# One weight stream for the delta rule's inputs, queries and keys, splits traced one unit ahead, and the decay chain traced in pieces

## The chip, the cores and the metric

The kernel runs on one core of one Trainium2 chip. Its time is the device time of one execution in microseconds (us), lower is better. The engines are named as the profile names them: PE (TensorE, matrix products), DVE (VectorE), ACT (ScalarE), POOL (GpSimd) and SP (SyncE, which only issues transfers here). Each engine works through its own instructions in order and waits on semaphores for the others.

## The reference

Two transformer blocks run after each other on 256 tokens of width 2048, all in float32. The change touches the first block alone:

```python
mod = silu(c) @ w_ada + b_ada                    # 6 vectors of 2048: shift, scale, gate, twice
h = rmsnorm(x, norm_mix) * (1 + sc_a) + sh_a
p = h @ w_in                                     # 2048 x 9296
c_q, c_kv, k_pe, q_g, k_g, v_g, z, b_logit, a_logit, gate_logits = split(p)
# latent attention, 8 heads
q = (rmsnorm(c_q) @ w_uq)                        # 512 x 8*(128+64), the last 64 of a head rotated
kv = (rmsnorm(c_kv) @ w_ukv)                     # 512 x 8*(128+128): keys and values
y_a = causal_attention(q, kv, rope(k_pe)) @ w_o_mla
# gated delta rule, 8 heads, chunks of 64 tokens
q, k, v = silu(causal_conv4(concat(q_g, k_g, v_g)))
beta = sigmoid(b_logit); g = -exp(A_log) * softplus(a_logit + dt_bias); G = cumsum(g) in each chunk
u, w = solve(I + strict_lower(beta * k k^T * exp(G_i - G_j)), [beta * v, beta * k * exp(G)])
S_next = S * exp(G_last) + (k * exp(G_last - G))^T (u - w S); o = (q * exp(G)) S + attn (u - w S)
y_b = (rmsnorm(o) * silu(z)) @ w_o_gdn
x = x + gt_a * ((sigmoid(gate_a) * y_a + sigmoid(gate_b) * y_b) @ w_o)
h = rmsnorm(x, norm_ffn) * (1 + sc_f) + sh_f
x = x + gt_f * ((silu(h @ w_gate) * (h @ w_up)) @ w_down)      # hidden width 5632
```

The second block (convolution and neighbourhood attention, then a feed-forward part of width 8192) follows.

## The kernel before

**Tiles.** Activations are kept with features on the 128 partitions and 256 tokens along the row, as two halves HI and LO whose sum is the float32 value. Weights come as units of 128x1024 float32 (512 KB). `Stream.load` (line 255) issues the transfer of a unit into one of 6 buffers named `raw`; `Stream.ahead` splits it: ACT rounds it to `hi` (line 268), DVE subtracts to get `lo` (line 269). There are 3 `hi` and 3 `lo` buffers for all streams together. `Stream.next` hands out slices of a unit; when a unit is used up it splits the next one there and then, unless one is ready, and calls `pump`. A product of 128 output features takes one 128-wide slice for each 128 inputs, so a unit holds 8 such slices; `mm` (lines 289 to 291) makes three products of 256 columns from a slice, `mm2` (lines 302 to 305) one of 512 and one of 256.

**Order.** The program is traced as straight code. A scheduler then orders the instructions of each engine: among those that it holds ready it takes what was traced first, and a transfer takes a free buffer in the order in which transfers were traced. Two helpers set the trace order. `merge` runs several generators side by side: each yields a cost, and the one with the lowest sum goes next. `pump` advances a list of fillers by a rate per weight unit. The fillers make the modulation vectors: `ada_pe` on PE (line 413) for the first two vectors while the first product runs, `ada_vec` (line 433) for the others, on ACT (line 440), DVE (line 441) and POOL (line 443), from weights in `raw` buffers. One step of `ada_vec` handles one 512 KB unit.

**Stages that the change touches.** (1) The start: 20 products of ones (line 506), the inputs, and the first modulation. (2) The first product, lines 519 to 550: 96 units of stream `wk` in six groups of input rows, with the modulation of a group made during the group before at a rate of its own (`RATE0`, line 38), and a `drain` at each group's start. (3) The logits of the decays (`proj(pm, wq, h)`, 2 units of `wq`), then the decay chain, lines 568 to 618: some 35 tiny instructions on PE, DVE and ACT, each fed by the one before. (4) Four sections, lines 1010 to 1020. Heads are handled in pairs: `pair_in` makes 6 convolved inputs of the delta rule (2 units of `wq` each), `pair_mid` the chunk matrices and their inverse by a chain of small products and DVE steps, `pair_out` the recurrence, `queries` the queries and keys of the attention from streams `wuq` and `wuk`, `attend` the attention. Section 1 merges `pair_in(0)` with the latents (lines 852 to 864), the rotary tables, the values (stream `wuv`) and `queries(0)`; sections 2 to 4 merge `pair_mid(i)`, `pair_out(i-1)`, `pair_in(i+1)`, `queries(i+1)` and the attention of pair i. (5) The output products (streams `woab` and `wo`), with fillers at rate 1.1 (`RATES[4]`), and the first group of the feed-forward product (stream `wgu`) with the last four `ada_vec` at rate 0.62.

A pair's inputs `kq` also sit in a `raw` buffer, from `pair_in` to the end of `pair_mid`.

## Time and profile before

| | us |
|---|---|
| median of 3 runs | 2780.33 (2779.88 to 2781.22) |
| the profiled execution | 2776.44 |
| its span, first to last instruction | 2774.7 |

The chip's profiler records every instruction of one execution. A *window* sums the busy time of each engine in a stretch of the span. *Waits* say which engine sat idle before an instruction and which other instruction ended the wait. The *timeline* lists instructions in order of time. TensorE's clock has two levels, 2.4 and 1.2 GHz; the profile gives the granted share, 1.00 and 0.50, and a window's mean of it. Times are us from the span's start unless marked ns. A number behind an x counts instructions.

### The profile page before, as it was taken

How to read it: one execution, taken by the hardware profiler on the slowest of the kernel's cores; microseconds unless marked ns; L12 is line 12 of the kernel's file. 1: busy time of each engine (PE TensorE's matmuls, PEld its weight loads, DVE VectorE, ACT ScalarE, POOL GpSimd, SP SyncE). 2: the span in 40 equal slices, each digit the busy share in tenths (PEclk: the TensorE clock that was granted, in tenths of full speed). 3: DMA queues.
4: the chain of work that ended last, by engine and by line, in shares of the span. 5: the costliest groups of instructions: out<-in, count | busy, mean ns of one | idle time of the engine just before them, and what ended most of it. 6: DMA issues, size and time to landing. Idle time of an engine off the chain costs nothing.

```text
span 2774.7 us, 42925 instructions
## 1 busy us (share of the span) xinstructions
PE 2677.4 (96%) x16226; PEld 2275.6 (82%) x16226; DVE 1941.0 (70%) x3066; ACT 1379.0 (50%) x2218; POOL 361.1 (13%) x310
## 2 busy tenths in 40 slices
PE   8999989899989999999999999999989999999997
PEld 5667867777777888888888889888978888888886
DVE  4865687778787877666666689796776566665665
ACT  5334565556554655344434564456554444453453
POOL 0000032223243122000000040000450000000012
PEclk9999989999999999999999999999999999999999
DMA  8795765548787687555555555544545555555553
GB/s 307 275 348 194 256 218 189 170 143 276 268 285 259 212 274 265 189 189 186 190 188 189 189 183 183 190 153 136 184 136 190 190 188 190 187 189 190 189 190 122
DMA packets 171279, 572.19 MB, mean 206 GB/s; under 512 B 19008, under 2 KB 19264, under 8 KB 171072
## 3 DMA queue, kind: packets, MB, share of 16 engines
q1 hardware_dynamic: 164736, 557.92, 59.5%
q10 hardware_dynamic: 6336, 11.53, 1.2%
q8 instruction: 128, 2.10, 0.3%
q14 instruction: 79, 0.65, 0.1%
HBM read 563.07 MB, written 6.29 MB: 205 GB/s over the span
## 4 chain that ended last, share of the span: by engine, by line
PE 78%; DVE 8%; DMA 5%; ACT 3%; issue 3%; POOL 2%; SPq 0%; ACTq 0%; DVEq 0%; POOLq 0%
PE ps L303 17%; PE ps L302 17%; PE ps L305 17%; PE ps L324 4%; PE ps L325 4%; PE ps L326 4%; PE ps L291 3%; PE ps L289 3%; PE ps L290 3%; DVE lo L269 3%; DMA raw<-ada 3%; PE O L426 1%; ACT hi L268 1%; DMA raw<-adaf 1%; DVE raw L441 1%
## 5 line engine op out<-in xcount | busy, mean ns | idle before, releaser
L269 DVE TENSOR_TENSOR lo<-raw,hi 128x1024 fp32r<-128x1024 f32 x856 | 1086.3, 1270 | 453.0 <-ACT hi L268 438.9
L268 ACT ACTIVATE hi<-raw 128x1024 fp32r<-128x1024 f32 x856 | 904.6, 1057 | 787.7 <-PE ps L305 442.1
L303 PEld LDWEIGHTS ps<-H,lo 128*128 128x128 f32 x2816 | 531.2, 189 | 139.2 <-DVE lo L269 21.8
L303 PE MATMUL ps<-H,lo 128*128 128x256 f32 x2816 | 576.5, 281 | 13.1 <-DVE lo L269 12.7
L302 PE MATMUL ps<-H,hi 128*128 128x512 f32 x1408 | 561.9, 400 | 15.5 <-DVE H L340 7.2
L305 PE MATMUL ps<-H,hi 128*128 128x512 f32 x1408 | 557.6, 397 | 0.1
L303 PEld LDWEIGHTS ps<-G,lo 128*128 128x128 f32 x1968 | 369.1, 188 | 92.1 <-DVE lo L269 7.1
L303 PE MATMUL ps<-G,lo 128*128 128x256 f32 x1968 | 389.7, 279 | 5.1 <-DVE lo L269 5.1
L305 PE MATMUL ps<-G,hi 128*128 128x512 f32 x984 | 388.7, 396 | 0.0
L302 PE MATMUL ps<-G,hi 128*128 128x512 f32 x984 | 386.9, 396 | 0.4 <-DVE Y L1056 0.4
L302 PEld LDWEIGHTS ps<-H,hi 128*128 128x128 f32 x1408 | 269.0, 191 | 22.7 <-DVE H L340 8.2
L377 POOL TENSOR_TENSOR acc<-acc,th 128x256 f32<-128x256 f32 x90 | 106.9, 1195 | 1318.4 <-ACT th L380 1317.4
L443 POOL TENSOR_TENSOR ada<-ada,raw 128x512 f32<-128x512 f32 x112 | 182.0, 1625 | 720.9 <-DVE raw L441 601.8
L305 PEld LDWEIGHTS ps<-H,hi 128*128 128x128 f32 x1408 | 265.7, 189 | 2.9 <-DVE H L340 0.3
L302 PEld LDWEIGHTS ps<-G,hi 128*128 128x128 f32 x984 | 187.0, 190 | 1.7 <-issue 0.7
L305 PEld LDWEIGHTS ps<-G,hi 128*128 128x128 f32 x984 | 184.8, 188 | 1.0
L324 PE MATMUL ps<-hi,H 128*128 128x512 f32 x448 | 175.7, 401 | 3.5 <-ACT hi L268 2.9
L325 PE MATMUL ps<-lo,H 128*128 128x512 f32 x448 | 177.0, 395 | 1.1 <-DVE lo L269 1.1
L326 PE MATMUL ps<-hi,H 128*128 128x512 f32 x448 | 175.8, 392 | 0.0
L289 PE MATMUL ps<-H,hi 128*128 128x256 f32 x528 | 151.5, 287 | 0.0
L291 PE MATMUL ps<-H,lo 128*128 128x256 f32 x528 | 151.4, 287 | 0.0
L290 PE MATMUL ps<-H,hi 128*128 128x256 f32 x528 | 151.4, 287 | 0.0
(394 smaller groups left out, 3384.5 us busy)
## 6 DMA issues: line engine op xcount, KB each, us to landing
raw<-wdn SPq DMA_DIRECT2D x216, 512.0 KB, 3.3
raw<-wgu SPq DMA_DIRECT2D x176, 512.0 KB, 3.3
raw<-wup SPq DMA_DIRECT2D x128, 512.0 KB, 3.3
raw<-wk SPq DMA_DIRECT2D x96, 512.0 KB, 5.2
raw<-ada SPq DMA_DIRECT2D x96, 512.0 KB, 4.5
raw<-wo SPq DMA_DIRECT2D x64, 512.0 KB, 4.2
Y<-ada SPq DMA_DIRECT2D x112, 256.0 KB, 5.6
raw<-wq SPq DMA_DIRECT2D x50, 512.0 KB, 4.3
```

The costliest lines, as they stand in the source:

```text
L268: S.activation(hi[:, sl], raw[:, sl], AF.Copy)
L269: V.tensor_tensor(lo[:, sl], raw[:, sl], hi[:, sl].bitcast(F32), op=ALU.subtract)
L289: PE.matmul(out, wh, x[:, HI], start=first, stop=False)
L290: PE.matmul(out, wh, x[:, LO], start=False, stop=False)
L291: PE.matmul(out, wl, x[:, HI], start=False, stop=last)
L302: PE.matmul(out, wh, x, start=first, stop=False)
L303: PE.matmul(out[:, LO], wl, x[:, HI], start=False, stop=last and wide)
L305: PE.matmul(out, wh, x, start=False, stop=last)
L324: PE.matmul(out, x[:, h], wh, start=(i == 0), stop=False)
L325: PE.matmul(out, x[:, h], wl, start=False, stop=False)
L326: PE.matmul(out, x[:, l], wh, start=False, stop=(i == n - 1))
L443: G.tensor_tensor(s, s, a0, op=ALU.add)
```

## The change

- **One stream.** The weights of the query and key products (`w_uq`, the key half of `w_ukv`) are laid into the array of `wq`, behind the delta rule's inputs of the same pair of heads, in the order of use. Streams `wuq` and `wuk` are gone. In each section `queries` follows `pair_in` in one chain; in section 1 the chain is `pair_in(0)`, `values`, `queries(0)`, and beside it run the latents, the decay chain and the rotary tables.
- **One ahead.** When `Stream.next` takes up a unit and no other is ready, it traces the split of the next unit at once. That holds for all streams.
- **Fillers.** `ada_pe` and `ada_vec` trace the transfer of their next weights one step earlier. The first product has one rate, 0.85 steps per unit, for all groups, and at a group's start only so many steps are forced as its inputs need. `RATES[4]` goes from 1.1 to 1.0. The last four `ada_vec` run with `shared=False`: two DVE instructions a step, none on ACT and POOL.
- **Decays.** The decay chain becomes a generator with ten yields, merged into section 1.
- The 20 products of ones are removed.

```diff
-RATE0 = (1.7, 1.3, 1.3, 1.25, 1.25)
+RATE0 = 0.85
-RATES = (0.85, 0.85, 0.62, 1.8, 1.1, 3.5, 4.2, 2.3)
+RATES = (0.85, 0.85, 0.62, 1.8, 1.0, 3.5, 4.2, 2.3)
...
                 self.hi, self.lo = self.ready.pop(0)
                 self.i = 0
+                if not self.ready and self.u < self.src.shape[0]:
+                    self.ahead()
                 pump()
...
-    def ada_vec(stream, chunks):
+    def ada_vec(stream, chunks, shared=True):
...
             w = stream.unit()
+            if stream.u < stream.src.shape[0] and k < KT - 2:
+                stream.prefetch(1)
             a0, a1 = w[:, :512], w[:, 512:]
-            S.activation(a0, a0, AF.Copy, scale=cact[:, k:k + 1])
-            V.scalar_tensor_tensor(a0 if k else s, a1, cact[:, k + 1:k + 2], a0, op0=ALU.mult, op1=ALU.add)
-            if k:
-                G.tensor_tensor(s, s, a0, op=ALU.add)
+            c0, c1 = cact[:, k:k + 1], cact[:, k + 1:k + 2]
+            if shared:
+                S.activation(a0, a0, AF.Copy, scale=c0)
+                V.scalar_tensor_tensor(a0 if k else s, a1, c1, a0, op0=ALU.mult, op1=ALU.add)
+                if k:
+                    G.tensor_tensor(s, s, a0, op=ALU.add)
+            else:
+                if k:
+                    V.scalar_tensor_tensor(s, a0, c0, s, op0=ALU.mult, op1=ALU.add)
+                else:
+                    V.tensor_scalar(s, a0, c0, None, op0=ALU.mult)
+                V.scalar_tensor_tensor(s, a1, c1, s, op0=ALU.mult, op1=ALU.add)
...
-    warm = ps("ps")
-    for i in range(20):
-        PE.matmul(warm[:, :P], ones, ones, start=True, stop=True)
...
     for gi, ks in enumerate(KGROUPS):
-        drain()
+        while len(h) <= ks[-1]:
+            step()
...
-        if gi + 1 < len(KGROUPS):
-            nx = KGROUPS[gi + 1]
-            filler.append(ada_group(nx))
-            rate[0] = (4 * len(nx) if nx[0] < NS else 3 * len(nx)) / (6 * len(ks)) * RATE0[gi]
+            for nx in KGROUPS[1:]:
+                filler.append(ada_group(nx))
+            rate[0] = RATE0
...
-    wuv, wuq, wuk = Stream("wuv", 512), Stream("wuq"), Stream("wuk")
+    wuv = Stream("wuv", 512)
...
-        merge(pair_in(0), chain(latents(), rotary_tables(), shared_key(), values(), queries(0, todo[0])))
+        merge(chain(pair_in(0), values(), queries(0, todo[0])), latents(), decays(), chain(rotary_tables(), shared_key()))
...
-    merge(pair_mid(0), pair_in(1), *[attend(*t) for t in todo[0]], queries(1, todo[1]))
-    merge(pair_mid(1), pair_out(0), pair_in(2), *[attend(*t) for t in todo[1]], queries(2, todo[2]))
-    rate[0] = RATES[1]
+    merge(pair_mid(0), chain(pair_in(1), queries(1, todo[1])), *[attend(*t) for t in todo[0]])
+    merge(pair_mid(1), pair_out(0), chain(pair_in(2), queries(2, todo[2])), *[attend(*t) for t in todo[1]])
...
-        filler.append(ada_vec(ada1, [32 + 4 * q + i for i in range(4)]))
+        filler.append(ada_vec(ada1, [32 + 4 * q + i for i in range(4)], False))
```

How instructions stand on the engines around three places follows. A row is a line of the program, the operation, what it writes and reads (numbers are buffers), and the shape; the changed kernel's lines are its own.

PE behind the first product, before: the last slices of the second pair of `wq` units, then the decay chain's products and the transposes of the latents (L861).

```order
L302 MATMUL ps_3008<-H_1999,hi_3068 128x512
L303 MATMUL ps_3008<-H_1999,lo_3069 128x256
L303 MATMUL ps_3008<-H_2024,lo_3069 128x256
L305 MATMUL ps_3008<-H_2024,hi_3068 128x512
L596 MATMUL ax_2977<-g,const 128x16
L597 MATMUL ax_2977<-g,ones 128x16
L599 MATMUL ax_2980<-g,ones 128x16
L861 MATMUL ax_3034<-const,kk_177 128x128
L861 MATMUL ax_3034<-const,kk_178 128x128
```

The same place in the changed kernel (L885 is the transpose, L592 the first product of the decay chain):

```order
L307 MATMUL ps_2944<-H_1528,hi_2947 128x512
L308 MATMUL ps_2944<-H_1528,lo_2948 128x256
L885 MATMUL ax_2976<-const,kk_156 128x128
L592 MATMUL ax_2982<-const,Z_2922 128x128 x2
L885 MATMUL ax_2976<-const,kk_157 128x128
L885 MATMUL ax_2999<-const,kk_156 128x128
L885 MATMUL ax_2999<-const,kk_157 128x128
L308 MATMUL ps_2944<-H_1553,lo_2948 128x256
L310 MATMUL ps_2944<-H_1553,hi_2947 128x512
L885 MATMUL ax_3016<-const,kk_156 128x128
L885 MATMUL ax_3016<-const,kk_157 128x128
```

Before, 20 small products stood in a row behind the fourth unit; now they stand between slices of the fourth and fifth unit, and L596's successor comes after the fifth.

ACT at the same place, before: the split of the fourth unit (L268), then the decay chain (L575 to L582).

```order
L268 ACTIVATE hi730_3068<-raw729_3066 128x1024
L440 ACTIVATE raw732_3072<-raw732_3072,cact_69 128x512
L568 ACTIVATE Z708_2946<-ps704_2887 128x256
L575 ACTIVATE beta_2953<-lg_2951 128x16
L580 ACTIVATE ex_2957<-ab_2955 128x16
L582 ACT_TABLE_LOAD
L582 ACTIVATE ln_2959<-u_2958 128x16
L637 ACTIVATE th739_3113<-ps716_3008 128x256
```

In the changed kernel:

```order
L271 ACTIVATE hi713_2947<-raw712_2945 128x1024
L449 ACTIVATE raw715_2951<-raw715_2951,cact_69 128x512
L449 ACTIVATE raw734_3035<-raw734_3035,cact_69 128x512
L580 ACTIVATE Z707_2922<-ps703_2866 128x256
L271 ACTIVATE hi732_3031<-raw731_3029 128x1024
L612 ACTIVATE sm752_3125<-vec_63 128x8
L344 ACTIVATE Y722_2979<-ax721_2976,vec_63 128x256
L594 ACTIVATE beta_2925<-lg_2924 128x16
```

One more split, that of the fifth unit (hi732), stands ahead of the chain. The split after it stands 22 rows further down, behind the last table load, as the fifth unit's did before (24 rows).

PE in section 2, before: steps of `pair_mid` (L745 to L755) and of the attention (L947 to L956) of the first pair.

```order
L751 MATMUL ax_4041<-yi_3981,G_3941 64x64 x8
L755 MATMUL ax_4041<-G_3941,yi_3981 64x64 x8
L947 MATMUL ax_4074<-const,sa_3950 128x128 x2
L947 MATMUL ax_4079<-const,sa_3958 128x128 x2
L745 MATMUL ax_4087<-G_4058,G_3718 64x64 x8
L953 MATMUL ax_4099<-tx_3765,Y_3314 128x128
L954 MATMUL ax_4099<-tx_3765,Y_3314 128x128
```

In the changed kernel, the same steps (L769 to L779, L971):

```order
L769 MATMUL ax_3880<-G_3838,G_3696 64x64 x8
L307 MATMUL ps_3905<-H_854,hi_3862 128x512
L308 MATMUL ps_3905<-H_854,lo_3863 128x256
L308 MATMUL ps_3905<-H_883,lo_3863 128x256
L310 MATMUL ps_3905<-H_883,hi_3862 128x512
L307 MATMUL ps_3905<-H_1080,hi_3862 128x512
L775 MATMUL ax_3916<-yi_3879,G_3838 64x64 x8
L779 MATMUL ax_3916<-G_3838,yi_3879 64x64 x8
L308 MATMUL ps_3905<-H_1080,lo_3863 128x256
L971 MATMUL ax_3952<-const,sa_3847 128x128 x2
```

Products of the next pair's inputs (L307 to L310) now stand between steps that stood next to each other.

## Rows read from the trace of the kernel before

**Rows 1.** Windows: stretch, length; PE, PEld, DVE, ACT, POOL busy; clock, DMA share, GB/s.

```profile
27.30:343.80 316.50, 314.15 (x1458) 224.30 (x1458) 208.65 (x283) 136.66 (x171) 1.38 (x1) 1.00 0.76 267
355.60:375.40 19.80, 10.99 (x39) 7.31 (x40) 15.16 (x40) 13.82 (x25) 3.69 (x4) 0.57 0.14 44
375.40:666.70 291.30, 268.64 (x2120) 225.08 (x2120) 231.02 (x462) 173.85 (x434) 87.81 (x88) 0.98 0.59 200
666.70:897.00 230.30, 216.67 (x1311) 177.85 (x1309) 186.81 (x283) 120.97 (x194) 87.11 (x57) 0.99 0.77 274
908.00:1090.00 182.00, 176.66 (x1004) 150.63 (x1003) 149.29 (x194) 106.10 (x165) 43.45 (x28) 1.00 0.78 260
1090.00:1600.00 510.00, 510.00 (x2933) 445.06 (x2932) 315.56 (x401) 232.96 (x305) 2.31 (x2) 1.00 0.58 191
```

**Rows 2.** Timeline of PE, 340 to 400 us: start, us, line, shapes [idle before].

```profile
369.90 0.80 PE L302 MATMUL ps<-H,hi 128*128 128x512 f32 x1 [4.72 <-ACT hi L268]
```

**Rows 3.** Timeline of ACT, the same stretch.

```profile
346.77 1.06 ACT L268 ACTIVATE hi<-raw 128x1024 fp32r<-128x1024 f32 x1 [0.65 <-PE ps L290]
...
366.81 1.28 ACT L646 ACT_TABLE_LOAD   x1
...
368.81 1.04 ACT L268 ACTIVATE hi<-raw 128x1024 fp32r<-128x1024 f32 x1
```

**Rows 4.** Timeline of DVE, the same stretch.

```profile
346.91 0.16 DVE L348 TENSOR_SCALAR sm<-sm 128x4 f32<-128x4 f32 x1
...
369.88 1.23 DVE L269 TENSOR_TENSOR lo<-raw,hi 128x1024 fp32r<-128x1024 f32 x1 [0.44 <-ACT hi L268]
```

**Rows 5.** Waits of PE, 375.4 to 666.7 us: us in total, times, longest.

```profile
PE ps L303 <- DVE lo L269: 6.3, 8, 1.6
...
PE ps L291 <- DVE lo L269: 2.1, 3, 1.1
...
PE ps L302 <- ACT hi L268: 1.4, 1, 1.4
```

**Rows 6.** Waits of ACT, the same stretch.

```profile
ACT hi L268 <- PE ps L305: 16.8, 8, 4.3
```

**Rows 7.** Waits of PE, 666.7 to 897 us.

```profile
PE ps L303 <- DVE lo L269: 5.1, 4, 2.7
```

**Rows 8.** Waits of PE, 908 to 1090 us.

```profile
PE ps L303 <- DVE lo L269: 5.3, 9, 1.3
```

**Rows 9.** Groups of DVE by shape, 908 to 1090 us: busy, mean ns | idle before.

```profile
L269 DVE TENSOR_TENSOR lo<-raw,hi 128x1024 fp32r<-128x1024 f32 x61 | 90.2, 1479 | 9.0 <-ACT hi L268 8.0
L441 DVE SCALAR_TENSOR_TENSOR raw<-raw,cact 128x512 f32<-128x512 f32 x28 | 21.1, 752 | 16.8 <-ACT raw L440 16.8
L1093 DVE TENSOR_TENSOR tx<-tx,tx 128x256 f32<-128x256 f32 x15 | 11.8, 788 | 0.4
```

**Rows 10.** The same groups, 1200 to 1500 us.

```profile
L269 DVE TENSOR_TENSOR lo<-raw,hi 128x1024 fp32r<-128x1024 f32 x108 | 132.4, 1225 | 75.7 <-ACT hi L268 72.8
...
L1093 DVE TENSOR_TENSOR tx<-tx,tx 128x256 f32<-128x256 f32 x19 | 8.1, 425 | 0.7
```

**Rows 11.** Waits of ACT, 908 to 1090 us.

```profile
ACT raw L440 <- DMA raw<-ada: 47.0, 24, 4.2
```

**Rows 12.** Transfers, the page's part 6: KB each, median us from issue to landing.

```profile
raw<-wq SPq DMA_DIRECT2D x50, 512.0 KB, 4.3
```

**Rows 13.** Windows, the start: columns as in rows 1.

```profile
13.00:16.00 3.00, 2.70 (x26) 1.51 (x24) 1.34 (x8) 0.00 (x0) 0.00 (x0) 1.00 1.06 402
17.00:27.30 10.30, 7.27 (x25) 4.81 (x25) 3.78 (x8) 5.04 (x9) 0.00 (x0) 0.50 1.04 414
```

**Rows 14.** Timeline of PE: three small products, at the start and in section 1.

```profile
13.65 1.05 PE L389 MATMUL ax<-ones,H 128*128 128x1 f32 x8
...
19.12 1.01 PE L451 MATMUL ax<-vec,ada 128*128 128x1 f32 x4 [0.50 <-ACT ada L429]
...
386.47 1.05 PE L451 MATMUL ax<-ones,ada 128*128 128x1 f32 x8 [0.81 <-POOL ada L443]
```

More of the change, by code (lines that the diff above doesn't have):

```diff
@@ L411, in emit, with ada_pe @@
     cact = one("cact", (P, 16))
-    def ada_pe(stream, chunks):
+    def ada_pe(stream, chunks, more=False):
         n = P * len(chunks)
@@ L419, in ada_pe @@
                 yield
-            w = []
-            for g in range(4):
-                if n * g % stream.size == 0:
-                    w.append(stream.unit())
+            need = 4 * n // stream.size
+            w = [stream.unit() for _ in range(need)]
+            if k + 4 < KT or more:
+                stream.prefetch(need - len(stream.early))
             for g in range(4):
@@ L498, in ada_group @@
             for k in ks[::2]:
[L499 removed]
+                yield from ada_pe(ada0, [16 + k, 17 + k, k, k + 1], k < KT - 2)
                 for i in (k, k + 1):
@@ L959, in queries @@
         p = ps("ps")
-        yield from proj_g(p, wuq, lat[0])
+        yield from proj_g(p, wq, lat[0])
         t, qp = tl("ca"), tl("qk")
@@ L965, in queries @@
             p = ps("ps")
-            yield from proj_g(p, wuq, lat[0])
+            yield from proj_g(p, wq, lat[0])
             qn = tl("s2")
@@ L969, in queries @@
             p = ps("ps")
-            yield from proj_g(p, wuk, lat[1])
+            yield from proj_g(p, wq, lat[1])
             kn = tl("s2")
```

114 lines of the change are left out of this document (63 added, 51 removed).

## The prediction

> **What bounds the kernel now.** I read the windows first. In every stretch PE has the most busy time, and from 1090 to 1600 us it has no idle time at all [rows 1]: there the change can win nothing, and all that is in it must come out of PE's idle time, or of its slower clock, elsewhere. The windows give the idle time as length less busy time: 2.4 us in the first product (27.3 to 343.8), 8.8 in the 19.8 us of the decay chain, 22.7 in the rest of the four sections up to 666.7, 13.6 in the output products, 5.3 in the first feed-forward group. No other engine fills its windows: DVE is busy for 231.0 of the sections' 291.3 us, 79%. So PE waits for results that come late, not for an engine that is full, and the order decides.
>
> The timelines show the large hole. PE stands still before 369.90 us for 4.7 us, for ACT's `hi` of the fifth unit of `wq` [rows 2]. That split stands in ACT's queue behind the whole decay chain and table loads, the last of which ends at 368.1; the split before it ran at 346.77 [rows 3]. DVE spends 346.91 to 369.88, 23.0 us, on the chain, the latents and the rotary tables before its half of the split [rows 4]. The clock's mean over this hole is 0.57 [rows 1]: at levels 1.00 and 0.50 that is 17.0 of 19.8 us at 1.2 GHz. In the sections the waits name the splits again: 6.3, 2.1 and 1.4 us, 9.8 in all [rows 5], and ACT for its part waited 16.8 us for PE to release a `hi` buffer [rows 6]. Three half-used units of `wq`, `wuq` and `wuk` can hold all three pairs of buffers; the next unit is then split only when one of them is used up, and PE waits for two engines in a row.
>
> **The change part by part.** The sum is made against the profiled execution, 2776.44 us; the median lies 3.9 above it.
>
> *Start.* Without the products of ones, PE comes to the eight products of the token sums (line 389) without having worked. They now take 1.05 us at clock 1.00 [rows 13, 14]; a product of that form took 1.01 us for four at 0.50 and 1.05 for eight at 1.00 [rows 14], so at 0.50 the eight take 2.1. They head the chain to the first modulation, so this counts in full: +1.0. From 17.0 to 27.3 us the clock was at 0.50 anyway [rows 13], so the later start costs nothing more. Bounds: 0, if the chain waits for its weights anyway, and +5.1, priced under the rivals.
>
> *First product.* The same `ada_pe` steps are spread evenly: 46 steps at 0.85 need 54 of the 60 units in which they must be done, and the tightest group has 10.2 steps traced for 10. PE has 2.4 us of idle time to give back; I take 0, with a bound of -2.4.
>
> *Decay chain.* The order shows one more split, the fifth unit's, ahead of the chain on ACT, and 22 rows later the sixth's. DVE has 71 rows where it had 64 before the split behind the chain, so that split comes where the fifth's was, near 369 us, and PE has used up one more unit by then. A unit is 16 products; 2933 products in 510.0 us [rows 1] make 2.8 us a unit. The latents' transposes now fall between slices and cover part of the rest. Back to back at half clock PE worked from 369.9 to the end of the window at 375.4; at full clock that is 2.7 us less, if the shorter hole keeps the clock up. Together -5.5. Bounds: 0, if DVE's seven added rows cost what the cover gives, and -11.5, the whole idle time and the clock.
>
> *One stream, one ahead, in the sections.* No instruction of PE or DVE goes; of the 9.8 us of waits for splits [rows 5] those go whose split now stands a unit earlier. Behind a removed wait DVE, 79% busy, may be late with the next step of the inverse's chain, so I take two thirds: -6.5, bounds -3.3 and -9.8. The remaining 12.9 us of idle time are waits for that chain and for the attention; the order puts products between its steps, but they were ready work before as well, so I count 0 there.
>
> *Clock in the sections.* Mean 0.98 over 291.3 us [rows 1] is about 12 us at half speed, which cost 6. These stretches follow the idle spots; I take a third, -2.0, bounds 0 and -6.
>
> *Output products.* Waits for splits are 5.1 us [rows 7]. Splitting ahead and the lower filler rate go against them, but transfers are dense here, 274 GB/s [rows 1]. Half: -2.5, bounds 0 and -5.1.
>
> *First feed-forward group.* Without POOL's additions DVE's subtraction should take 1225 instead of 1479 ns and line 1093's product 425 instead of 788: the first column is with POOL at work, the second without [rows 9, 10]. That frees 61 x 0.254 + 15 x 0.363 = 20.9 us of DVE. The second DVE instruction of 32 steps costs 32 x 0.752 = 24.1 [rows 9]. So DVE's load stays, 149 to 152 of 182 us, but without subtractions twice as long as usual, right behind which PE waits. Of 5.3 us [rows 8] I take half: -2.7. A bound above zero: ACT now waits 47.0 us in 24 steps for these weights to land [rows 11]; that wait moves to DVE, where the splits queue behind it. The transfer traced a step earlier should take most of it away; what is left, and DVE's 3.2 us more, may cost +3.
>
> *Starts of the two feed-forward products.* There the inputs are made tile by tile on DVE, and a split that now comes earlier stands ahead of one of them: about 1.2 us [rows 10] at two places, half of it covered: +1.0, bounds 0 and +2.
>
> Sum: 1.0 - 5.5 - 6.5 - 2.0 - 2.5 - 2.7 + 1.0 = -17.2. That gives 2759.2 for a profiled execution and 2763.1 for the median.
>
> **The rivals.** *DVE is next.* If the waits only change their names, because DVE at 79% is late with the chain once splits go first, a third of the sections' gain stays (-3.3), one unit at the hole without the clock (-2.8), and nothing in stages behind: with +1.0 and +1.0 that is -4.1, 2776. For it: the change takes no DVE work out of the sections. Against it: PE's waits name splits in 9.8 of 22.7 us. The changed order does what the text says at the places I looked at, so a change without effect is in this case too.
>
> *A cold clock.* For 10.3 us after the start the clock was at 0.50 [rows 13]. If it rises later by as long again, because nothing has run before, PE works 10.3 us more at half speed, 5.1 us: 2768. The Trainium skill (TensorE: Matmul & The Clock Gate, "Part 1: The HAM clock gate") says that the throttled level is the default and that only activity releases it. This speaks against taking the products of ones out. By that rule the start costs 5.1 us instead of 1.0; the trace has the clock fall to 0.50 soon after those products, so that their effect was gone when the first weights came.
>
> *More than the waits.* If all waits for splits, the whole hole and the slow clock go: 1.0 - 11.5 - 9.8 - 6.0 - 5.1 - 5.3 + 1.0 = -35.7, 2745.
>
> *Raw buffers: slower.* Six `raw` buffers serve the weights, the fillers and, for most of a section, two `kq` tiles. A filler's unit transferred a step early holds a buffer longer, so a weight's load starts later. A load takes 4.3 us to land [rows 12]; from the point at which it is issued less than that before its split's turn, ACT waits with all that is queued behind, the decay and softmax steps too. Fillers lose 2.0 us a step in this way now (47.0 / 24, [rows 11]). If a fifth of the 64 units of the sections, 13, lost as much, that is +26 against -17: 2789. For it: transfers to these buffers are always waiting for a release. Against it: a section uses a unit in some 5 us (291.3 us for about 57 units), so three buffers are enough.
>
> **How the numbers follow.** Forecast 2763 with a chance of 0.52 (2752 to 2773 by its own bounds); more than the waits 0.13; cold clock 0.11; DVE next 0.14; raw buffers 0.10. The range from 2747 to 2778 leaves out half of the second case, the fourth's upper end and the last. A measurement of this kernel can tell about 0.2%, 5.6 us, from no change: faster means below 2774.8, slower above 2785.9. Forecast, more and cold clock are faster: 0.76. DVE next is the same: 0.14. Raw buffers are slower: 0.10.
>
> **What would show it.** Right: in the changed profile the stretch behind the first product has under 6 us of idle time and a mean clock above 0.8; waits for splits in the sections are under 4 us; line 269's successor has a mean near 1225 ns in the first feed-forward group; the first main product starts about 1 us later. Wrong: DVE waits for transfers in the feed-forward group, ACT's `hi` waits for `raw` of `wq`, or the sections' idle time stays near 22 us under other names.

## The result and the profile after

| | before | after |
|---|---|---|
| time, median (lowest to highest), us | 2780.1 (2772.8 to 2781.2) | 2755.8 (2753.9 to 2758.9) |
| profiled execution's span, us | 2774.7 | 2752.6 |
| PE busy, us | 2677.4 | 2664.6 |
| POOL busy, us | 361.1 | 316.0 |

The ratio is 0.9919, with a 95% interval of 0.9899 to 0.9939: 24.3 us less by the medians, 22.1 by the spans. A second set of runs of the changed kernel gave 2755.7 us and 0.9912 (0.9898 to 0.9926).

The windows of the changed kernel answer to [rows 1]. The columns are the same: stretch, length; PE, PEld, DVE, ACT, POOL busy; clock, DMA share, GB/s. The stretches are the first product, the decay chain, the rest of the sections, the output products and the first feed-forward group.

```profile
27.90:343.00 315.10, 313.04 (x1460) 223.67 (x1459) 207.35 (x281) 135.02 (x170) 0.00 (x0) 1.00 0.75 268
355.00:375.40 20.40, 14.55 (x65) 11.35 (x66) 17.79 (x52) 13.08 (x25) 5.04 (x6) 0.68 0.28 92
375.40:651.70 276.30, 264.69 (x2111) 222.46 (x2110) 229.84 (x458) 173.57 (x430) 90.04 (x87) 0.98 0.61 208
651.70:884.00 232.30, 217.26 (x1307) 177.43 (x1305) 196.17 (x283) 121.45 (x199) 86.78 (x57) 0.99 0.79 274
894.80:1069.00 174.20, 173.92 (x1005) 151.65 (x1004) 149.00 (x226) 87.50 (x133) 0.00 (x0) 1.00 0.81 273
```

Length less PE's busy time gives the idle time: 2.1 us in the first product (2.4 before), 5.9 at the decay chain (8.8), 11.6 in the sections (22.7), 15.0 in the output products (13.6), 0.3 in the feed-forward group (5.3). POOL has nothing left to do in the last row.

The waits of PE follow, as us in total, times, longest: first in the sections (375.4 to 651.7), then in the output products (651.7 to 884.0), then in the feed-forward group (894.8 to 1069.0).

```profile
PE ax L958 <- DVE th L924: 2.6, 1, 2.6
PE ax L922 <- ACT ca L986: 2.2, 3, 1.4
PE ps L330 <- DVE lo L272: 2.1, 1, 2.1
...
PE ps L308 <- DVE lo L272: 0.7, 2, 0.5
...
PE ps L329 <- ACT hi L271: 0.3, 1, 0.3
```

```profile
PE ax L1057 <- DVE H L1053: 2.9, 2, 1.9
PE ps L308 <- DVE lo L272: 2.8, 4, 1.1
PE ax L466 <- POOL ada L452: 2.1, 2, 1.9
PE ps L307 <- DVE H L1052: 2.0, 1, 2.0
PE ps L307 <- DVE Y L1079: 1.3, 1, 1.3
```

```profile
PE ps L307 <- DVE tx L1111: 0.2, 1, 0.2
```

In the kernel before, the same tables hold these lines besides those of [rows 5] (the first one) and [rows 7] (the others):

```profile
PE ps L289 <- ACT hi L268: 1.1, 1, 1.1
```

```profile
PE ax L1034 <- DVE H L1030: 2.8, 2, 1.6
PE ax L451 <- POOL ada L443: 2.3, 2, 1.5
PE ps L325 <- DVE lo L269: 1.3, 2, 0.7
```

Waits for splits (`lo`, `hi`) are 3.1 us in the sections, against 10.9 before (the 9.8 of [rows 5] and the 1.1 above). In the output products they are 2.8 us against 6.4 (5.1 in [rows 7], and 1.3). Lines 1057 and 466 wait there as long as their counterparts did before (lines 1034 and 451). In the feed-forward group the 5.3 us of [rows 8] are gone.

The groups of DVE in the feed-forward group (894 to 1075 us: busy, mean ns | idle before) answer to [rows 9].

```profile
L272 DVE TENSOR_TENSOR lo<-raw,hi 128x1024 fp32r<-128x1024 f32 x63 | 76.8, 1221 | 11.9 <-ACT hi L271 11.5
L458 DVE SCALAR_TENSOR_TENSOR ada<-raw,cact,ada 128x512 f32<-128x512 f32 x32 | 23.9, 747 | 0.4
L455 DVE SCALAR_TENSOR_TENSOR ada<-raw,cact,ada 128x512 f32<-128x512 f32 x28 | 21.0, 749 | 9.0 <-DMA raw<-ada 8.7
```

The subtraction's mean fell from 1479 to 1221 ns. Of the 47.0 us for which ACT waited for these weights [rows 11], 8.7 are left, now on DVE.

**Where the time went, by main products.** PE works through 13,984 main products (those into `ps`, the products of ones not counted) in about the same order in each kernel. The following table is worked out from the traces: the time from the start of one numbered main product to that of another, in us. The numbers are 0, 1152, 1280, 2240, 2624, 3136, 3200 and 4200; in the kernel before they start at 22.7, 343.8, 381.3, 657.9, 789.4, 892.6, 913.6 and 1100.2 us. All experiments stand in it.

```
            to      first    decay    sections  last sec.,  output    norm   first FF  rest   span
            no. 0   product  chain              output 1    products         group
before       22.7   321.2    37.5     276.6     131.4       103.2     21.0   186.7     1674.4 2774.7
earlyonly    23.2   321.3    38.3     271.0     135.5       105.0     20.5   188.8     1674.1 2777.8
after        23.9   319.1    36.2     263.7     133.6       102.9     21.0   178.7     1673.4 2752.6
again        23.3   318.6    36.0     263.7     134.1       102.2     21.0   178.9     1676.0 2753.7
ones         23.8   318.6    36.0     263.6     133.9       103.0     20.6   178.7     1675.6 2753.8
pool         23.5   318.6    36.0     263.7     132.2       103.3     19.8   186.5     1673.8 2757.3
late         23.4   322.6    39.3     269.2     130.9       103.3     20.1   178.3     1674.1 2761.2
whole        23.4   319.2    39.3     264.3     134.2       103.0     20.5   178.7     1675.9 2758.4
noearly      23.8   319.5    35.9     269.1     134.9       111.1     21.0   178.5     1676.1 2769.8
rates        23.4   317.3    37.7     264.0     134.6       104.7     21.0   179.5     1674.6 2756.8
pace         23.3   319.7    37.1     263.5     135.0       103.4     20.1   178.7     1674.9 2755.7
dvelate      23.3   318.7    35.8     263.7     131.1       103.2     20.3   178.8     1675.1 2749.9
both         23.6   318.0    37.0     262.7     128.7       102.9     21.0   178.7     1673.5 2746.2
alldve       25.6   318.9    33.7     252.1     136.8       101.3     20.6   178.8     1674.8 2742.5
```

The rows "after" and "again" are the same kernel. Up to the feed-forward group their stages differ by 0.7 us at most; the rest, 61% of the time, by 2.6. Kernels that differ from them elsewhere agree about as well (263.5 to 264.0 us in the sections of `ones`, `pool`, `rates` and `pace`), except in the stretch behind the sections, where `pool` and `pace` take 132.2 and 135.0. So I put a stage that moved by 2 us or more down to the edit, in that stretch 3 us, and the span's last few us say nothing. Of the kernel before there is one profile; how its stages differ from execution to execution is not known. From before to after, 12.9 us went in the sections, 8.0 in the first feed-forward group, 2.1 in the first product and 1.3 at the decay chain; the start lost 1.2 and the stretch behind the sections 2.2.

### The profile page after: what moved, and what is told of

Same layout as the page of the kernel before. It is cut to its first block, busy times and chain, and to the rows that moved or that the text cites. A ratio compares the mean times of both kernels' runs of the same rounds, so it can differ in the third digit from the quotient of the medians.

```text
span 2752.6 us, 42684 instructions
## 1 busy us (share of the span) xinstructions
PE 2664.6 (97%) x16186; PEld 2267.7 (82%) x16186; DVE 1949.0 (71%) x3098; ACT 1358.0 (49%) x2185; POOL 316.0 (11%) x282
## 4 chain that ended last, share of the span: by engine, by line
PE 82%; DVE 8%; DMA 4%; issue 3%; ACT 2%; POOL 1%; SPq 0%; ACTq 0%; DVEq 0%; POOLq 0%
PE ps L307 18%; PE ps L310 18%; PE ps L308 18%; PE ps L330 4%; PE ps L329 4%; PE ps L331 4%; PE ps L294 3%; PE ps L296 3%; PE ps L295 3%; DVE lo L272 3%; DVE raw L450 1%; DMA raw<-wo 1%; PE O L431 1%; ACT hi L271 1%; DMA raw<-adaf 1%
## 5 line engine op out<-in xcount | busy, mean ns | idle before, releaser
L272 DVE TENSOR_TENSOR lo<-raw,hi 128x1024 fp32r<-128x1024 f32 x856 | 1071.8, 1255 | 463.0 <-ACT hi L271 451.5
L307 PE MATMUL ps<-H,hi 128*128 128x512 f32 x1408 | 562.5, 401 | 13.0 <-DVE H L345 7.6
L310 PE MATMUL ps<-H,hi 128*128 128x512 f32 x1408 | 559.2, 398 | 0.1
L307 PE MATMUL ps<-G,hi 128*128 128x512 f32 x984 | 388.4, 396 | 3.3 <-DVE H L1052 2.0
L310 PE MATMUL ps<-G,hi 128*128 128x512 f32 x984 | 388.2, 396 | 0.0
L307 PEld LDWEIGHTS ps<-H,hi 128*128 128x128 f32 x1408 | 269.4, 191 | 20.1 <-DVE H L345 8.6
L310 PEld LDWEIGHTS ps<-H,hi 128*128 128x128 f32 x1408 | 266.4, 189 | 3.3 <-DVE H L345 0.3
L452 POOL TENSOR_TENSOR ada<-ada,raw 128x512 f32<-128x512 f32 x84 | 138.3, 1647 | 587.4 <-DVE sm L353 344.9
L307 PEld LDWEIGHTS ps<-G,hi 128*128 128x128 f32 x984 | 186.7, 190 | 5.0 <-DVE H L1052 2.3
L310 PEld LDWEIGHTS ps<-G,hi 128*128 128x128 f32 x984 | 184.4, 187 | 1.0
```

The lines of the kernel that those rows point to most:

```text
L272: V.tensor_tensor(lo[:, sl], raw[:, sl], hi[:, sl].bitcast(F32), op=ALU.subtract)
L307: PE.matmul(out, wh, x, start=first, stop=False)
L310: PE.matmul(out, wh, x, start=False, stop=last)
L452: G.tensor_tensor(s, s, a0, op=ALU.add)
```

## The experiments

The median times, and the ratios to the kernel before that ran beside them:

```
           median (lowest to highest)       ratio    95% interval
again      2755.7 (2751.3 to 2757.3)        0.9912   0.9898 to 0.9926
ones       2756.0 (2755.0 to 2757.8)        0.9922   0.9904 to 0.9941
pool       2767.8 (2759.1 to 2772.1)        0.9961   0.9948 to 0.9974
late       2762.5 (2760.0 to 2763.0)        0.9942   0.9927 to 0.9958
whole      2760.6 (2758.4 to 2763.5)        0.9938   0.9921 to 0.9955
noearly    2768.6 (2763.7 to 2775.2)        0.9974   0.9962 to 0.9986
rates      2755.2 (2750.3 to 2758.6)        0.9920   0.9902 to 0.9938
pace       2756.5 (2755.6 to 2757.4)        0.9926   0.9913 to 0.9939
dvelate    2751.2 (2749.1 to 2755.7)        0.9909   0.9893 to 0.9924
earlyonly  2777.5 (2768.3 to 2781.8)        0.9989   0.9978 to 1.0001
both       2748.1 (2747.1 to 2755.4)        0.9892   0.9875 to 0.9908
alldve     2743.4 (2740.5 to 2749.8)        0.9872   0.9855 to 0.9889
```

**again: the changed kernel once more.**

> The changed kernel once more, for a second profile and more times beside the kernels that are compared with it. Expected: 2753 to 2759 us, and stage times that differ from its first profile by up to 1 us where nothing but chance differs; what is larger in other kernels' stages may then be read as their edit.

As expected; the 1 us of the expectation holds for the stages up to the end of the first feed-forward group.

**ones: the products of ones back.**

```diff
+    warm = ps("ps")
+    for i in range(20):
+        PE.matmul(warm[:, :P], ones, ones, start=True, stop=True)
     start = ada_group(KGROUPS[0])
```

> The changed kernel with the twenty products of ones put back at the start; all else is as in the changed kernel. Theory (the ones only warm the engine for the first small products): the first main product starts at 22.7 us instead of 23.9, and the end moves by the same 1.2 us, to about 2754.6 by the median. Rival (the ones cost something later, since the changed kernel's rows show a clock of 1.00 where the kernel before had 0.50 from 17.0 to 27.3 us): the clock falls to 0.50 again and the first product's end comes up to 5 us later, so 2756 to 2761. By the theory the main products between 23 and 28 us take 0.63 us each in both kernels, whatever the window's clock says.

Neither: the first main product starts at 23.8 us, between the 23.3 and 23.9 of the two profiles without the ones, and the time is the same (it lies at the rival's 2756, but the first product ends no later: at 342.4 us, against 343.0 and 342.0). The timeline of PE shows why (start, us, line, shapes, count [idle before]).

```profile
11.53 1.16 PE L431 MATMUL O<-G,cact 128*32 128x256 f32 x8 [3.28 <-DMA G<-adas]
...
13.97 1.87 PE L394 MATMUL ax<-ones,H 128*128 128x1 f32 x8
```

The windows of these two stretches (clock third from the end):

```profile
11.50:14.00 2.50, 2.10 (x11) 0.48 (x11) 0.96 (x2) 0.00 (x0) 0.00 (x0) 0.84 1.05 394
14.00:17.00 3.00, 3.00 (x20) 2.32 (x22) 0.95 (x6) 0.00 (x0) 0.00 (x0) 0.50 1.04 416
```

Here too the eight small products took 1.87 us, as at half clock, and not the 1.05 of [rows 14], though the ones had run: between them PE had waited 3.28 us for the first weights. In `earlyonly`, which has the ones as well, they took 1.87 us too. So the kernel before seems to have met them at full clock by chance, in the one execution that was profiled. Kernels without the ones reach the first main product at 23.3 to 25.6 us, so a start of 23.9 is within chance.

**pool: the last four ada vectors through POOL again.**

```diff
-        filler.append(ada_vec(ada1, [32 + 4 * q + i for i in range(4)], False))
+        filler.append(ada_vec(ada1, [32 + 4 * q + i for i in range(4)]))
```

> The changed kernel with the last four ada vectors made by ACT, DVE and POOL again, their load still traced a step early. Theory (POOL's additions slow DVE's subtractions, and PE waits behind those): the subtraction's mean goes from 1221 back to about 1480 ns in the first feed-forward group, PE's idle time there from 0.3 to about 5, and the time rises by 6 to 8 us, to 2762 to 2764. Rival (the early load was what helped, because ACT no longer waits 47.0 us for the weights): the group stays within 2 us of the changed kernel's 181.0 us, 2756 to 2758.

The theory holds for the stage. The first feed-forward group takes 186.5 us, as before, although the load stands a step early. The median rises by 12 us, more than the 7.8 of the stage and more than the 6 to 8 expected; the profiled execution was the fastest of the eight, and what the slower ones lost in addition no trace shows. Its window of that group, and DVE's groups (894 to 1082 us):

```profile
897.00:1083.50 186.50, 181.56 (x1033) 154.87 (x1032) 152.26 (x199) 107.45 (x166) 44.16 (x28) 1.00 0.79 266
```

```profile
L272 DVE TENSOR_TENSOR lo<-raw,hi 128x1024 fp32r<-128x1024 f32 x63 | 90.3, 1439 | 12.4 <-ACT hi L271 12.4
...
L1116 DVE TENSOR_TENSOR tx<-tx,tx 128x256 f32<-128x256 f32 x16 | 13.7, 864 | 0.5
```

DVE is as busy as without POOL (152.3 of 186.5 us, 151.4 of 178.8 in the changed kernel); it is the length of the single subtraction, 1439 ns against 1221, that PE waits behind. The Trainium skill (SBUF — State Buffer, "Who interferes with whom") says that a DVE instruction with two SBUF inputs contends with a GpSimd instruction that reads SBUF. The rows agree: with POOL at work this subtraction is 18% longer in the mean. Taken one by one, 22 of the 63 subtractions in `pool` overlap one of POOL's additions in time; they take 1847 ns in the mean and up to 2355. The other 41 take 1208 to 1228 ns, as without POOL. So it is the overlap that lengthens them.

**late: no split one unit ahead.**

```diff
                 self.i = 0
-                if not self.ready and self.u < self.src.shape[0]:
-                    self.ahead()
                 pump()
```

> The changed kernel without the split one unit ahead: with one stream, the next unit is split only when the last one is used up. Theory (splits that come too late were PE's waits in the sections): PE waits for splits 8 to 10 us in the sections and about 5 in the output products, and the time rises by 10 to 13 us, to 2766 to 2769. Rival (one stream in one chain is what helped, the order of products having changed with it, and the split ahead does little): the time stays within 4 us, below 2760, and the split's waits in the sections stay under 4 us.

Between the two: 6.7 us slower by the medians, 8.6 by the spans. PE's waits in the sections (375 to 655 us) read:

```profile
PE ax L920 <- ACT ca L984: 5.5, 3, 3.5
PE ps L306 <- DVE lo L272: 3.0, 6, 0.9
PE ax L957 <- POOL qk L924: 2.7, 2, 1.9
...
PE ps L328 <- DVE lo L272: 1.0, 2, 0.6
```

Without the split ahead the waits for splits are about 4 us, not 8 to 10: most of the 10.9 of the kernel before had gone already with the other edits. Yet the sections take 5.5 us longer than in the changed kernel; PE waits longer for ACT and POOL instead (`ca` 5.5 us against 2.2, `qk` 2.7 against 1.3: the queries' chain). The first product, where I had expected nothing of the split, takes 3.5 us longer, the decay chain's stretch 3.1. Behind the sections, in the first stretch of the output products, it is 2.7 us shorter: there the split ahead may cost something, though kernels that are alike there differ by as much.

**whole: the decay chain in one piece.**

```diff
-        merge(chain(pair_in(0), values(), queries(0, todo[0])), latents(), decays(), chain(rotary_tables(), shared_key()))
+        for _ in decays():
+            pass
+        merge(chain(pair_in(0), values(), queries(0, todo[0])), chain(latents(), rotary_tables(), shared_key()))
```

> The changed kernel with the decay chain traced whole ahead of the merge, and the latents, the rotary tables and the shared key in one chain again. Theory (the pieces let PE do one more unit in the hole and little else): the hole behind the first product has 2 to 4 us more idle time, the rest of the sections is unchanged, and the time rises by 2 to 4 us, to 2758 to 2760. Rival (the pieces, by the order they give to section 1, are behind much of the 14 us that the sections gained): the time rises by 8 us or more, to 2764 and above.

The theory holds in the main: 3.1 us more in that stretch, where the hole has 9.8 us of idle time (355 to 378 us) against 5.9, and 0.6 in the sections. By the medians it is 4.8, a little over the 2 to 4 expected. The stretch is as long as in `late`, 39.3 us, and no shorter than the 37.5 of the kernel before: neither the pieces nor the split ahead gains there without the other.

**noearly: the vectors' load not a step early.**

```diff
             w = stream.unit()
-            if stream.u < stream.src.shape[0] and k < KT - 2:
-                stream.prefetch(1)
```

> The changed kernel with the load of the next half-row of weights in the ada vectors traced with its own step again, not a step early; the last four vectors stay on DVE. Theory (the load a step early keeps DVE from waiting for transfers with the splits behind it): in the first feed-forward group DVE waits 15 to 30 us for these transfers instead of 8.7, PE is idle for 2 to 5 us instead of none, and the time rises by 2 to 5 us, to 2758 to 2761. Rival (DVE has room there, with 152 of 181 us busy, so the wait costs nothing): within 1.5 us of the changed kernel.

Neither: the time is 12.8 us longer by the medians, but not where the theory had it. In the feed-forward group DVE waits 8.3 us for these transfers, as in the changed kernel, and the group stays at 178.5 us: there the rival is right. The loss is 5.4 us in the sections and 8.2 in the output products, where PE's first wait (783 to 894 us) and the window read:

```profile
PE ax L464 <- POOL ada L450: 7.5, 3, 4.2
```

```profile
783.20:894.30 111.10, 101.62 (x546) 86.94 (x545) 86.05 (x98) 54.31 (x72) 54.63 (x35) 0.94 0.75 264
```

The small product at the end of an ada vector stands in PE's queue behind the vector's last step. Weight, ACT, DVE and POOL come in a row ahead of it. The longest of the three waits, on ACT, POOL and PE in this order:

```profile
827.30 0.72 ACT L447 ACTIVATE raw<-raw,cact 128x512 f32<-128x512 f32 x1 [3.63 <-DMA raw<-ada]
```

```profile
836.53 2.12 POOL L450 TENSOR_TENSOR ada<-ada,raw 128x512 f32<-128x512 f32 x1 [0.68 <-POOL acc L382]
```

```profile
838.71 1.87 PE L464 MATMUL ax<-ones,ada 128*128 128x1 f32 x8 [4.25 <-POOL ada L450]
```

ACT had waited 3.63 us for the vector's weights; from there POOL works with pauses of 0.7 us until the last addition ends at 838.65, and PE, which had reached the small product, stands still for 4.25 us. In this window the clock's mean is 0.94 instead of 1.00. With the load a step early this wait is 0.2 us in that stretch. In the sections PE's longest waits are those of `late`, for `ca` (4.8 us) and `qk` (2.6); how the late load causes these was not followed.

**earlyonly: the kernel before with that one edit.**

```diff
             w = stream.unit()
+            if stream.u < stream.src.shape[0] and k < KT - 2:
+                stream.prefetch(1)
```

> The kernel before with one edit: the load of the next half-row of weights in the ada vectors traced a step early; POOL still adds. Theory (the early load repairs what the split one ahead does to the vectors' steps, which stand behind it on ACT and DVE, and gives little by itself): ratio to the kernel before 0.998 to 1.000, PE's waits for POOL's last addition in the output products go from 3 us to under 2. Rival (late loads of the vectors cost the kernel before as much as they cost the changed one): 10 us or more faster, ratio 0.996 or less, the sections' end and the output products shorter by 5 us each.

By the time the theory holds: 0.9989, and the interval takes in 1. The stages tell it in more detail, with a caution: the two profiled executions differ by 3.1 us, the medians by 2.1 the other way, so some 5 us of the stages' differences are chance. In the sections the early load gains 5.6 us by itself, as much as it costs to take it away from the changed kernel (5.4). In the next two stretches this profile is 4.1 and 1.8 us longer, and 2.1 in the feed-forward group. Beside the splits ahead those losses don't show: there the early load gains 1.3 and 8.2 (`noearly`).

**rates: the old rates and drains in the first product.**

```diff
-RATE0 = 0.85
+RATE0 = (1.7, 1.3, 1.3, 1.25, 1.25)
...
-        while len(h) <= ks[-1]:
-            step()
+        drain()
```

(and the old line for `rate[0]` at each group)

> The changed kernel with the old rates of the first product's modulation and the drain at each group; all else changed. Theory (at an even pace the modulation's products stand in fewer groups between the main products): PE's time from the first main product to the last of the first product rises by 1.5 to 2.5 us and its idle time by no more than 0.5; the time rises by about 2 us, to 2758. Rival (the 2 us that this stage gained come from elsewhere, the split one ahead first of all): within 0.5 us of the changed kernel in this stage.

Neither: the first product gets 1.3 to 1.8 us shorter with the old rates, the decay chain's stretch 1.5 to 1.7 longer, and the time is the same. In `both`, with the same rates, the first product is shorter by 0.6 to 1.1 us. PE's idle time there is 1.0 and 1.2 us with the old rates and 2.0 to 2.1 with the even pace. So the first product's gain is the split one ahead (3.5 in `late`), and the even pace gives a part of it back, 0.6 to 1.8 us.

**pace: the pieces of the decay chain counted double.**

```diff
-        yield 1.5
+        yield 3.0
```

(all nine of them in `decays`)

> The changed kernel with each piece of the decay chain counted at 3.0 instead of 1.5 in the merge, so that more of the first pair's products stand between the pieces. Theory (PE stands still in the hole because its products are traced ahead of the chain's end): PE's idle time behind the first product falls from about 8 to 4 to 6 us and the time by 2 to 4 us, to 2752 to 2754. Rival (the products that come between need splits from ACT and DVE, which the chain then waits for, and all of section 1 waits for the chain): the idle time moves into section 1 and the time stays, or rises by up to 3 us.

The rival, as far as the time goes: the stretch is 1 us longer, no more than chance, and the time the same.

**dvelate, both, alldve: more ada vectors on DVE alone.** `dvelate` takes four more, those of the output products; `both` adds the old rates; `alldve` takes all sixteen.

```diff
-        filler.append(ada_vec(ada1, [64 + 4 * q + i for i in range(4)]))
+        filler.append(ada_vec(ada1, [64 + 4 * q + i for i in range(4)], False))
```

```diff
-    def ada_vec(stream, chunks, shared=True):
+    def ada_vec(stream, chunks, shared=False):
```

> The changed kernel with four more of the ada vectors on DVE alone, the four that run in the output products. Theory (POOL's additions slow DVE's subtraction to a mean of 1517 ns between 652 and 884 us, and PE waits behind it): the mean falls to about 1300, PE's idle time there falls from 13.6 to 6 to 9 us, and the time falls by 4 to 7 us, to 2749 to 2752. Rival (DVE is busy 83% of this stage and takes 32 more instructions of 0.75 us, 24 us, while it saves 65 times 0.2 us, 13): the idle time stays and the time is the same or up to 4 us longer.

Between the two: the subtraction's mean between 652 and 884 us fell as expected, from 1518 to 1292 ns, but PE's idle time in the two stretches of the output products only from 13.6 to 11.1 us. The median is 4.6 lower than that of the changed kernel, but the intervals of the two ratios overlap; by the stages 2.5 us went in the first stretch behind the sections, within what that stretch differs by chance.

> The changed kernel with the old rates and drains of the first product, and the four vectors of the output products on DVE alone. Theory (the old rates gain 1.8 us in the first product, and the four vectors 3 to 4 us in the output products; the parts lie far apart and add up): 2749 to 2751, 5 to 6 us below the changed kernel beside it. Rival (the credit that the old rates leave behind changes where the fillers of the sections fall, which gave the first product's gain back before): 2752 to 2755.

By the median 7.6 us below the changed kernel beside it, 2 more than the sum of the parts; the stages that differ are the first stretch behind the sections (128.7 against 134.1) and, within chance, the sections, by 1.0. The rates' gain in the first product was 0.6 here, against `again`, and the decay chain's stretch gave 1.0 back.

> The changed kernel with all sixteen ada vectors made by DVE alone; POOL has none of their additions left. Theory (where DVE has the next step of the inverse's chain to do, 32 us of added instructions in the sections cost more than the subtractions win, 59 times 0.1 us): the sections are 4 to 10 us longer, the output products 2 to 4 us shorter, the time 2756 to 2764. Rival (POOL's additions are what slows DVE everywhere, and PE waits less without them): sections shorter too, 2745 to 2750.

My theory fell, and in the direction: the time is 2743.4 us, 12.3 below the changed kernel beside it, and it is the sections that shrink, by 11.6 us. The window of the same main products, in the changed kernel and in this one:

```profile
379.20:642.90 263.70, 252.09 (x2031) 211.60 (x2030) 223.02 (x445) 163.54 (x396) 84.03 (x81) 0.98 0.60 203
```

```profile
378.20:630.30 252.10, 247.29 (x2032) 207.97 (x2031) 227.77 (x485) 137.25 (x353) 22.01 (x42) 1.00 0.63 211
```

DVE gets 40 more instructions and only 4.8 us more work, 90% of a shorter stretch; PE's idle time falls from 11.6 to 4.8 us and the clock's mean rises to 1.00. The groups of DVE in these windows show most of what pays for the added instructions, first in the changed kernel, then in this one.

```profile
L272 DVE TENSOR_TENSOR lo<-raw,hi 128x1024 fp32r<-128x1024 f32 x58 | 77.0, 1332 | 8.8 <-ACT hi L271 8.7
L668 DVE SCALAR_TENSOR_TENSOR s<-up,vec,s 128x256 f32<-128x256 f32 x69 | 47.1, 683 | 1.3 <-ACT s L666 0.8
```

```profile
L272 DVE TENSOR_TENSOR lo<-raw,hi 128x1024 fp32r<-128x1024 f32 x58 | 71.9, 1241 | 4.7 <-ACT hi L271 4.3
L668 DVE SCALAR_TENSOR_TENSOR s<-up,vec,s 128x256 f32<-128x256 f32 x69 | 34.1, 494 | 1.0 <-ACT s L666 0.8
```

69 steps of line 668, which I had not counted, get 13.0 us shorter, the subtractions 5.1. The stretch behind the sections is not shorter (136.8 us against 134.1). Three things change together here: DVE's own instructions are no longer stretched, PE no longer waits for POOL's last addition, and ACT loses 26 us of work. Which of them PE's 6.8 us of idle time owe is not told apart. `alldve` is faster than the kernel before and the changed kernel: its ratio to the kernel before is 0.9872 (0.9855 to 0.9889). With the old rates it was not tried.

## Why the prediction was right, and where not

The time of 2755.8 lies in the range, 7 us below the forecast, and faster was right. The mechanism was right in that the gain came out of PE's idle time: between the first main product and number 4200 it fell from 57.0 to 41.0 us. It was right for the feed-forward group too, and in part for the decay chain. In the sections, the largest term, the reason was not: the waits for splits went, but most of them without the split ahead, and they were not what the time went with. The sum was less right than its total, for errors cancelled. The terms beside what the stages of the two profiles show, in us:

```
term                          predicted (bounds)      measured
start                         +1.0 (0 to +5.1)        +1.2, within chance
first product                  0 (-2.4 to 0)          -2.1
decay chain                   -5.5 (-11.5 to 0)       -1.3
sections, splits              -6.5 (-9.8 to -3.3) )
sections, clock               -2.0 (-6.0 to 0)    )   -12.9
output products               -2.5 (-5.1 to 0)        +1.9
first feed-forward group      -2.7 (-5.3 to +3)       -8.0
starts of the FF products     +1.0 (0 to +2)           0.0 (the first)
rest                          0                       -1.0
sum                           -17.2                   -22.1
```

(The last section's end lies with the output products in the measured column, and the start of the second feed-forward product in the rest; the terms are rounded, and the sum is the difference of the spans.)

- **Start.** The size was right and the reason was not: the small products run at half clock with the products of ones too (`ones`). The cold-clock rival is out: the time with the ones is the same, and full speed came at 28 us, against 27.3 in [rows 13]. (Its 2768 also counts the 5.1 us on top of the 1.0 that they replace; in its place they give 2767.) The Trainium skill (TensorE: Matmul & The Clock Gate, "Part 1: The HAM clock gate") states that the throttled level is the default and that activity releases it. The trace of `ones` agrees: the clock was at 0.50 again from 14 to 17 us, when the small products ran. (In the kernel before it was still 1.00 from 13 to 16 us [rows 13].) By that rule alone the ones could have saved something; here they saved nothing.
- **First product.** I priced only the pace, at nothing, and overlooked that the split one ahead holds for this stream as well. It gains 3.5 us (`late`); the pace loses 0.6 to 1.8 of it (`both`, `rates`).
- **Decay chain.** The split itself came as the order showed: one more unit is done between the chain's small products, and the idle time of 5.9 us is what I said would show it. What failed is the clause "if the shorter hole keeps the clock up". ACT still has table loads and the chain's steps between two splits, so PE still waits, for 3.06 us where [rows 2] had 4.72, and then runs at half clock as before. ACT's timeline and PE's behind the hole:

```profile
349.25 1.05 ACT L271 ACTIVATE hi<-raw 128x1024 fp32r<-128x1024 f32 x1
...
365.34 1.28 ACT L636 ACT_TABLE_LOAD   x1
...
369.03 1.04 ACT L271 ACTIVATE hi<-raw 128x1024 fp32r<-128x1024 f32 x1
```

```profile
370.12 0.79 PE L307 MATMUL ps<-H,hi 128*128 128x512 f32 x1 [3.06 <-ACT hi L271]
...
375.36 0.63 PE L307 MATMUL ps<-H,hi 128*128 128x512 f32 x1
...
376.19 0.39 PE L310 MATMUL ps<-H,hi 128*128 128x512 f32 x1
```

  Main product 1248 starts at 370.1 us instead of 375.7, which is 5.6 us earlier, 4.8 of them won in this stretch. But full speed comes at 376 us, as in the kernel before (375.4), so the unit from 1248 to 1264 takes 6.3 us where it took 2.8 before (0.87 us of it is a wait for `lo`). That gives 3.5 of the 4.8 us back. The clock's mean rose only from 0.57 to 0.68, where I had asked for 0.8.

- **Sections.** Of 12.9 us, 5.6 came with the vectors' load a step early (`earlyonly`; 5.4 by `noearly`) and 5.5 with the split one ahead, on top of the rest (`late`). What lies between `earlyonly` and `late`, one stream, the pieces and the pace among it, is worth 1.8 us, which no run tells apart. Each figure is the difference of two profiles. I had priced the early load in the feed-forward group only, where it gives nothing, so one step that failed is "The remaining 12.9 us of idle time ... I count 0 there". The other is that the waits for splits go because the split stands a unit earlier. Between the same main products these waits are 10.9 us before, 8.3 in `earlyonly`, 3.3 in `late`, which has no split ahead, and 3.1 in the changed kernel. So most of them went with the one stream and the edits beside it, at a gain of 1.8 us, and the split ahead mostly took waits for the queries' chain. Why it does, and why `noearly` brings back the same two waits, stays open. The forecast's size, 9.8 us, also left out the wait of line 289. My -8.5 came near by missing one edit, giving another's gain a wrong reason, and taking the clock as a gain; its mean stayed at 0.98.
- **Output products.** The splits' waits fell by more than half (6.4 to 2.8 us), but PE's idle time did not (13.6 before, 15.0 after): new waits of line 307 for DVE's `H` (line 1052, 2.0 us) and `Y` (1.3 against 0.4), and some for the inverse's end, came in their place. In the first stretch the time rose by 2.2 us, about what `late` has less there (2.7), which is no more than chance. Without the early load the stage would have been 8.2 us longer still. The rival in which the waits only change names fits this stage best.
- **First feed-forward group.** Right mechanism, size a third: I halved 5.3 us of idle time, and all of it went, with 2.7 us more of PE's own time (181.3 us busy before, 178.5 after, for the same products; why is not shown). `pool` shows that making these vectors on DVE alone is behind it, since with the early load and POOL the stage is at 186.5; `noearly` shows that the early load is not needed there.
- **Raw buffers.** The sign of this rival is there and is small: in the sections ACT waits 6.9 us for transfers, while PE's waits for all splits are 3.1 us.

```profile
ACT hi L271 <- PE ps L310: 7.6, 9, 2.1
ACT hi L271 <- DMA raw<-wq: 6.9, 8, 2.4
```

  The first row was 16.8 us in [rows 6]: ACT now waits less for PE to release a buffer. In `alldve`, 10.1 us shorter by its span, ACT's wait for those transfers is 21.4 us, and the sections are the shortest of all.

## What to carry to other kernels

Price every edit in every stage that it runs in: the split ahead gained in the first product, and the early load in the sections and the output products, and I had priced neither there. A wait that goes is not yet time won: in the sections most waits for splits went with a gain of 1.8 us. A chain that ends on a queue of PE (load, ACT, DVE, POOL, then a small product) can become a wait of PE when its load is late (`noearly`), and the waits table names its last link, not the load. Work shared between DVE and POOL should be counted with what it adds to the DVE instructions that it overlaps: here the same vectors on DVE alone, with twice the instructions for it, were 12 us faster.

## What the runs showed of the hardware that I had not expected

POOL's additions lengthen more of DVE's instructions than the subtraction: line 668's step, 128x256 with two inputs and a scalar, took 683 ns in the sections with them and 494 without, more in proportion than the subtraction (1332 and 1241). One by one, the traces show that this goes by overlap in time. In the changed kernel 35 of these steps overlap no addition or product on POOL and take 470 to 486 ns; 34 overlap one and take 892 ns in the mean, up to 1522. In `alldve` all but two overlap none and take 466 to 486 ns. The vectors' own step of that kind (line 450, 128x512) goes the same way: in the sections it takes 734 to 752 ns where it overlaps none (37 steps) and 1251 in the mean where it does (6 steps). In the feed-forward group of `pool` none of the 32 overlaps one, so its mean there, 748 ns, is that of the same kind of step without POOL (747): POOL's addition waits for this very step.

The granted clock in the windows' rows is not to be trusted ahead of its first change. In the changed kernel it reads 1.00 from the start on, yet the first main products took 0.63 us, as they do at 0.50, and 0.40 from 28 us on:

```profile
25.77 0.63 PE L330 MATMUL ps<-lo,H 128*128 128x512 f32 x1
...
28.17 0.40 PE L330 MATMUL ps<-lo,H 128*128 128x512 f32 x1
```

The durations tell the level; with the ones, where the clock had changed before, the row from 17 to 23 us reads 0.50.
